# Weights ahead of bias rows in the first head pairs, two modulation chunks moved to the output projection, all copies of values on ScalarE

## The chip, the cores and the metric

One core of one Trainium2 chip runs the kernel. The metric is the device time of one execution in microseconds (us). All times below are in us unless they are marked otherwise. PE is TensorE (matrix products), DVE VectorE, ACT ScalarE, POOL GpSimd and SP SyncE, which here only issues transfers.

## The reference

A decoder trunk of two layers on 256 tokens of width 1024, with fp32 data and fp32 results. Layer 0 mixes tokens with dilated sliding-window attention, layer 1 with chunked gated linear attention; a gated convolutional FFN follows each. Every sub-layer is normalised and modulated by six vectors (shift, scale and gate, twice) that come from the conditioning vector c. The change lies in layer 0's attention:

```python
mod = jax.nn.silu(c) @ w_ada[i] + b_ada[i]
sh1, sc1, g1, sh2, sc2, g2 = [m[:, None, :] for m in jnp.split(mod, 6, axis=-1)]
h = rmsnorm(x, norm_mix[i]) * (1.0 + sc1) + sh1
qkv = (h @ w_in).reshape(B, S, A_GROUPS, 3, A_HEADS, A_HEAD_DIM)
# for each of 3 groups (window, dilation): scores + bias, mask, softmax, times values
wts = jax.nn.softmax(jnp.stack(lses), axis=0)
o = jnp.sum(wts[..., None] * jnp.stack(outs), axis=0)
x = x + g1 * (o.reshape(B, S, A_WIDTH) @ w_out)
```

The 16 heads are taken as 8 head pairs of 2 x 64 columns.

## The kernel before, in words

**Products.** An fp32 product is made of three fp32r products (`mm3`, lines 175 to 177): high part times high part, and the two mixed ones. So each weight tile, a `raw` of up to 128 x 2048 loaded by SyncE (line 159, 1 MB), is split: ScalarE casts the high part (`whi`, line 165), VectorE subtracts it to get the low part (`wlo`, line 169), each in two halves. There are four `raw` buffers and three pairs of split buffers, so a load starts when an older tile's split, or a chunk's dot products, have freed a buffer.

**Modulation chunks.** `next_ada` takes the next of the 40 chunks that are left at this point (`ada_chunk`): a 1 MB load (line 133) into a `raw` buffer, two dot products of 128 x 1024 on VectorE (line 138) and two small activations on ScalarE. The chunks are spread over the kernel: two after the first probabilities, one after each weight tile of queries, and so on.

**Pairs.** Eight tiles of weights hold the queries, keys and values of pair 0 and the queries and keys of pair 1, whose values have two tiles of their own. `evacuate` brings queries (`q`, ScalarE) and keys (`k`, VectorE, group 0 on both) out of PSUM, `by_group` the values `v` in four copies for each half of the tokens: for half 0 all on ScalarE, for half 1 the two big ones (lines 506 and 507) on VectorE. Then for each pair u from 2 on: three tiles of queries and keys (`queries`, PSUM tile `pqk`), two tiles of values (`values`, `pv`), `scores` (`s`), `probabilities` (bias and row maximum on VectorE in line 439, exponentials on ScalarE, normalised `pn` on VectorE), transposes of the four probability tiles (`turn`, `t`, copied to `pt` by ScalarE and VectorE in turn), and `outputs` (`po`, split into `ohi` and `olo`) of the pair before. Bias rows are loaded per pair by eight small transfers (`bias_of`, lines 347 and 348).

**Projection.** `project` multiplies the 8 pairs' outputs by w_out in four tiles (`py`). For the last pair, transposes and outputs stand among the products of the first two tiles (`between`).

**What sets the order.** The code gives each engine's instructions, and a scheduler orders them on each engine by when it expects their inputs; `behind(x)` holds an instruction behind x on its own engine's queue, `tc.issue_after` a transfer behind another. Each engine then runs its queue strictly in that order. SyncE's transfers go round eight semaphores: one that is issued waits for the landing of the one eight places before it. PSUM has eight banks in three tags: "p" two, "s" four, "t" two; `pqk` takes "p", `pv` "p", `s` "s", `t` and `po` "t". For the first two pairs the products take all eight.

Of the kernel before, what the change touches and what calls it, by code (L numbers as in the profile page):

```python
# [57 lines left out]
def trunk(ctx: ExitStack, tc: tile.TileContext, I, out):  # L58
# [337 lines left out]
    with tc.issue_after(last_load[0].ins):  # L396
        nc.sync.dma_start(x_all, I["xT"])
        nc.sync.dma_start(rows_d, rows)
        nc.sync.dma_start(small[:, C_CW:], I["small"][:, C_CW:])
# [59 lines left out]
    def turn(tiles, normed_p, pt):  # L459
        for i in tiles:  # L460
            t = bank("t", "t")
            for j in range(3):
                c = slice(P * j, P * j + P)
                nc.tensor.transpose(t[:, c], normed_p[i][:, c], ident)
            (nc.vector.tensor_copy if i % 2 else nc.scalar.copy)(pt[:, i, :], t[:, 0:KEYS])

# [18 lines left out]

    def evacuate(q, k, g, pq, pk):
# [3 lines left out]
        if g:  # L490
            nc.scalar.mul(q[g], pq, 0.125)
            return nc.vector.tensor_copy(k[g], pk)
# [8 lines left out]
    def by_group(v, pv, n):  # L501


        copy = (nc.scalar.copy, nc.vector.tensor_copy)[n]
# [3 lines left out]
        nc.scalar.copy(v[low, P : 2 * P], pv[top, 2 * P : 3 * P])  # L508
        nc.scalar.copy(v[top, 2 * P : 3 * P], pv[low, P : 2 * P])
# [22 lines left out]
    def queries(u, g, q, k):  # L532
        w = split(I["wqk"][u - 2, g], 2048)
        pqk = bank("pqk", "p")
# [11 lines left out]
    def by_groups(pv):  # L546
        v = [att.tile([P, NG * P], F32, tag=f"v{t}", name="v") for t in range(2)]
        for n in range(2):
            by_group(v[n], pv[n], n)
# [48 lines left out]
    before = probabilities(s, bias)  # L598

    for u in range(2, NPAIR):  # L600
        bias = bias_of(u)
        if u > 2:
            qk = new_qk()
            with behind(last):
                queries(u, 0, *qk)
        middle, end = queries(u, 1, *qk)
        with behind(middle):
            turn((0, 1), *before)
        with behind(end):
            turn((2, 3), *before)  # L610
# [5 lines left out]
        with behind(end):  # L616
# [17 lines left out]
    def project(src, o_of, l, sub, between=None):  # L634
# [32 lines left out]
        for n in range(4):  # L667
# [6 lines left out]
            leave(n, ps)  # L674
        return early
# [491 lines left out]
```

## Time and profile before

| | |
|---|---|
| three runs | 783.54 median, 782.6 to 784.26 |
| profiled execution, its own time | 783.19 |
| its span | 781.4 |
| PE busy | 760.2 (97%) |
| DVE busy | 640.4 (82%) |
| ACT busy | 479.4 (61%) |
| POOL busy | 12.4 (2%) |
| granted TensorE clock, mean of the span | 0.988 |
| bytes moved by DMA, mean rate | 186.30 MB, 238 GB/s |

A row of the timeline gives start, duration, engine, line, operation, the tiles written and read, their shapes and how many instructions it groups; in square brackets stands how long the engine was idle before it, and what ended that. The waits view adds up such idle time by what was waited for: us in total, times, longest. The windows view gives, for a stretch of the span, what each engine was busy, and the granted clock. The chain of waits is the chain of work that ended last, in order of time; SPq is SyncE issuing, DMA a transfer from issue to landing.

### The profile page before, as it was taken

The numbers are of one execution on the slowest core, as the hardware profiler recorded it, in microseconds if no ns is written. First come the engines' busy times: TensorE is split into PE (matmuls) and PEld (weight loads), VectorE is DVE, ScalarE is ACT, GpSimd is POOL, SyncE is SP. The second block draws the span as 40 slices with busy tenths as digits, with TensorE's granted clock in tenths as the row PEclk, the third lists the DMA queues.
The fourth block names the chain that finished last, engine by engine and source line by source line (L and its number), as shares of the span: only waits on it lengthen the run. The fifth ranks groups of instructions, "written<-read, shape, count | busy, mean of one in ns | idle before, by whom it ended". The sixth has DMA issues, their size and how long they took to land.

```text
span 781.4 us, 15909 instructions
## 1 busy us (share of the span) xinstructions
PE 760.2 (97%) x6416; PEld 734.3 (94%) x6416; DVE 640.4 (82%) x1152; ACT 479.4 (61%) x932; POOL 12.4 (2%) x36
## 2 busy tenths in 40 slices
PE   8997989999999999999999999999999999999997
PEld 5996979999999999999999998898999999999996
DVE  6997688788789958999998877797668898899662
ACT  5565455555646657866666656655667866667552
POOL 0000000000000010000000100000010000000000
PEclk9998999999999999999999999999999999999999
DMA  9988685776877746777745993966345665555651
GB/s 348 418 327 311 224 286 167 306 271 242 315 248 277 273 135 244 252 258 244 253 143 196 342 336 135 363 231 230 133 144 183 241 216 174 205 189 210 224 187 55
DMA packets 36200, 186.30 MB, mean 238 GB/s; under 512 B 8412, under 2 KB 10972, under 8 KB 19870
## 3 DMA queue, kind: packets, MB, share of 16 engines
q1 hardware_dynamic: 35744, 184.84, 66.0%
q8 instruction: 50, 0.82, 0.4%
q10 hardware_dynamic: 382, 0.45, 0.2%
q14 instruction: 24, 0.20, 0.1%
HBM read 184.17 MB, written 1.10 MB: 237 GB/s over the span
## 4 chain that ended last, share of the span: by engine, by line
PE 67%; DMA 15%; DVE 13%; ACT 3%; issue 1%; SPq 0%; ACTq 0%; DVEq 0%
PE pab L175 10%; PE pab L176 10%; PE pab L177 10%; DMA raw<-in_wqk 7%; DVE wlo L169 7%; PE pd L175 5%; PE pd L176 5%; PE pd L177 5%; DMA raw<-in_wv 4%; DVE ada_raw L138 3%; PE py L177 2%; PE py L176 2%; PE py L175 2%; ACT whi L165 2%; DMA bias<-rows_d 1%
## 5 line engine op out<-in xcount | busy, mean ns | idle before, releaser
L169 DVE TENSOR_TENSOR wlo<-raw,whi 128x1024 fp32r<-128x1024 f32 (+3 forms) x274 | 291.8, 1098 | 50.5 <-ACT whi L165 49.7
L165 ACT CAST whi<-raw 128x1024 fp32r<-128x1024 f32 (+3 forms) x274 | 245.6, 944 | 116.2 <-PE pab L176 41.3
L177 PE MATMUL pab<-hhi,wlo 128*128 128x256 f32 x672 | 184.9, 276 | 0.0
L176 PE MATMUL pab<-hlo,whi 128*128 128x256 f32 x672 | 184.8, 277 | 0.0
L175 PE MATMUL pab<-hhi,whi 128*128 128x256 f32 x672 | 183.4, 277 | 0.0
L175 PE MATMUL pqk<-hhi,whi 128*128 128x256 f32 x440 | 122.2, 289 | 7.1 <-ACT whi L165 4.2
L177 PEld LDWEIGHTS pab<-hhi,wlo 128*128 128x128 f32 x672 | 126.2, 188 | 0.0
L176 PEld LDWEIGHTS pab<-hlo,whi 128*128 128x128 f32 x672 | 126.0, 188 | 0.2
L175 PEld LDWEIGHTS pab<-hhi,whi 128*128 128x128 f32 x672 | 125.2, 188 | 0.1
L177 PE MATMUL pqk<-hhi,wlo 128*128 128x256 f32 x440 | 122.8, 284 | 1.0 <-DVE wlo L169 1.0
L176 PE MATMUL pqk<-hlo,whi 128*128 128x256 f32 x440 | 122.9, 283 | 0.0
L138 DVE CUSTOM_DVE_ANT_0 ada_raw<-ada_raw,c_bc 128x1024 f32<-128x1024 f32 x96 | 113.6, 1222 | 10.7 <-DMA ada_raw<-in_w_ada 10.7
L176 PE MATMUL pd<-glo,whi 128*128 128x256 f32 x352 | 97.1, 276 | 0.0
L177 PE MATMUL pd<-ghi,wlo 128*128 128x256 f32 x352 | 97.1, 276 | 0.0
L175 PE MATMUL pd<-ghi,whi 128*128 128x256 f32 x352 | 96.8, 276 | 0.0
L175 PEld LDWEIGHTS pqk<-hhi,whi 128*128 128x128 f32 x440 | 83.7, 195 | 8.6 <-ACT whi L165 4.5
L177 PEld LDWEIGHTS pqk<-hhi,wlo 128*128 128x128 f32 x440 | 84.2, 192 | 1.7 <-DVE wlo L169 1.3
L176 PEld LDWEIGHTS pqk<-hlo,whi 128*128 128x128 f32 x440 | 84.4, 192 | 0.1
L176 PEld LDWEIGHTS pd<-glo,whi 128*128 128x128 f32 x352 | 66.1, 188 | 0.0
L177 PEld LDWEIGHTS pd<-ghi,wlo 128*128 128x128 f32 x352 | 66.1, 188 | 0.0
L175 PEld LDWEIGHTS pd<-ghi,whi 128*128 128x128 f32 x352 | 65.9, 188 | 0.0
L728 ACT ACTIVATE r<-pab,small 128x256 f32<-128x256 f32 x86 | 46.7, 558 | 15.5 <-DVE r L731 15.4
(214 smaller groups left out, 1267.3 us busy)
## 6 DMA issues: line engine op xcount, KB each, us to landing
ada_raw<-in_w_ada SPq DMA_DIRECT2D x47, 1024.0 KB, 6.3
raw<-in_w_up SPq DMA_DIRECT2D x42, 1024.0 KB, 4.9
raw<-in_w_down SPq DMA_DIRECT2D x32, 704.0 KB, 5.5
raw<-in_wqk SPq DMA_DIRECT2D x18, 1024.0 KB, 7.8
raw<-in_wv SPq DMA_DIRECT2D x14, 768.0 KB, 4.4
raw<-in_w SPq DMA_DIRECT2D x7, 960.0 KB, 6.4
raw<-in_w_out_a SPq DMA_DIRECT2D x4, 1024.0 KB, 7.3
raw<-in_w_v_b SPq DMA_DIRECT2D x4, 1024.0 KB, 6.1
```

The costliest lines, as they stand in the source:

```text
L138: nc.vector.tensor_tensor_reduce(w, w, c_bc, op0=ALU.mult, op1=ALU.add, scale=1.0, scalar=0.0, accum_out=dot,)
L165: copied[0] = nc.scalar.copy(hi[:, c], raw[:, c])
L169: last_lo[0] = nc.vector.tensor_tensor(lo[:, c], raw[:, c], hi[:, c].bitcast(F32), op=ALU.subtract)
L175: mm(ps, a[0], b[0], start=start, stop=False)
L176: mm(ps, a[0], b[1], start=False, stop=False)
L177: return mm(ps, a[1], b[0], start=False, stop=stop)
L728: nc.scalar.activation(r, u[:, :T], AF.Identity, scale=cw[2], bias=col(C_CB + 44 * l + f))
```

## The change

1. The load of `x` (`x_all` from `xT`, 1 MB) moves from ahead of the first bias rows to behind pair 2's second tile of queries.
2. `by_group` makes all four copies of both halves on ScalarE.
3. After the products of pairs 0 and 1, the values are copied first; then queries and keys are evacuated, pair 0 and pair 1 interleaved.
4. The two chunks after the first probabilities go. Two are added in `project`, one after each of the first two tiles of layer 0's output projection; the 40 chunks keep their sequence, so those in between come two places later.
5. Pair 2's first tile of queries takes a PSUM bank of tag "t", its casts stand behind the last cast of the evacuation on ScalarE, and the bias rows of pairs 1 and 2 are issued behind weight tiles instead of ahead of them. The values of pair 1 are started before the bias rows of pair 0.
6. The transposes of pair 0 are taken in two halves around the scores of pair 1, and the scores of each pair from 2 on stand behind the last transpose.

```diff
-        nc.sync.dma_start(x_all, I["xT"])
...
-    def by_group(v, pv, n):
-        copy = (nc.scalar.copy, nc.vector.tensor_copy)[n]
+    def by_group(v, pv):
+        copy = nc.scalar.copy
...
-    def queries(u, g, q, k):
-        w = split(I["wqk"][u - 2, g], 2048)
-        pqk = bank("pqk", "p")
+    def queries(u, g, q, k, tag="p", after=()):
+        w = split(I["wqk"][u - 2, g], 2048, after=(after, after))
+        pqk = bank("pqk", tag)
...
+    qk0, qk1 = new_qk(), new_qk()
+    v = by_groups(pv)
+    for qk, pqk, g in ((qk0, pqk0, 0), (qk1, pqk1, 0), (qk0, pqk0, 1), (qk0, pqk0, 2), (qk1, pqk1, 1), (qk1, pqk1, 2)):
+        evacuate(*qk, g, pqk[2 * g], pqk[2 * g + 1])
+    pv = [bank("pv", "p") for _ in range(2)]
+    end = values(1, 0, pv)
     bias = bias_of(0)
-    qk0, qk1 = new_qk(), new_qk()
-    for g in range(NG):
-        evacuate(*qk0, g, pqk0[2 * g], pqk0[2 * g + 1])
-    v = by_groups(pv)
-    for g in range(NG):
-        evacuate(*qk1, g, pqk1[2 * g], pqk1[2 * g + 1])
-    pv = [bank("pv", "p") for _ in range(2)]
-    with behind(values(1, 0, pv)):
+    with behind(end):
         s, last = scores(*qk0)
...
-    for n in range(2):
-        next_ada()
-
-    bias = bias_of(1)
+
     qk = new_qk()
     with behind(last):
-        end = queries(2, 0, *qk)
+        end = queries(2, 0, *qk, tag="t", after=last_q)
+    bias = bias_of(1)
     with behind(end[1]):
-        turn(range(4), *before)
+        turn((0, 1), *before)
         s, last = scores(*qk1)
     with behind(last):
+        turn((2, 3), *before)
         outputs(0, v0, before[1])
...
     for u in range(2, NPAIR):
-        bias = bias_of(u)
         if u > 2:
+            bias = bias_of(u)
...
         middle, end = queries(u, 1, *qk)
+        if u == 2:
+            bias = bias_of(u)
+            with tc.issue_after(last_load[0].ins):
+                nc.sync.dma_start(x_all, I["xT"])
...
-            turn((2, 3), *before)
+            turned = turn((2, 3), *before)
...
-        with behind(end):
+        with behind(end, turned):
             s, last = scores(*qk)
...
             leave(n, ps)
+            if n < len(first):
+                next_ada()
```

SyncE's queue in the first pairs, before: the bias rows of pair 0 end, x among them, then two chunks and the first two of eight rows of pair 1, behind which pair 2's first tile of queries (`raw<-in_wqk`) comes.

```order
L348 DMA bias<-rows_d 64x2x64
L397 DMA x_all<-in_xT 128x2048
L347 DMA bias<-rows_d 64x258
L348 DMA bias<-rows_d 64x2x64
L133 DMA ada_raw<-in_w_ada 128x2048 x2
L347 DMA bias<-rows_d 64x258
L348 DMA bias<-rows_d 64x2x64
```

The same place on SyncE, with the change:

```order
L347 DMA bias<-rows_d 64x258
L348 DMA bias<-rows_d 64x2x64
L159 DMA raw<-in_wqk 128x2048
L133 DMA ada_raw<-in_w_ada 128x2048
L347 DMA bias<-rows_d 64x258
L348 DMA bias<-rows_d 64x2x64
```

Pair 2's first tile of queries stands directly behind pair 0's bias rows, with one chunk behind it (the chunk that belongs to that tile); before, eight bias rows of pair 1, two chunks and x stood ahead of it. x now stands behind the second tile.

VectorE while pairs 0 and 1 are evacuated, before: keys, two copies of values among them, then a chunk's dot products and the first probabilities.

```order
L492 COPY k<-pqk 128x256
L506 COPY v<-pqk 64x256
L507 COPY v<-pqk 64x2x128
L492 COPY k<-pqk 128x256
L495 SCALAR_TENSOR_TENSOR q<-pqk,q 128x256
L492 COPY k<-pqk 128x256
L499 TENSOR_TENSOR k<-pqk,k 128x256
L492 COPY k<-pqk 128x256
L499 TENSOR_TENSOR k<-pqk,k 128x256
L138 ISA ada_raw,dot<-ada_raw,c_bc 128x1024
```

The same place on VectorE, with the change:

```order
L497 SCALAR_TENSOR_TENSOR q<-pqk,q 128x256
L494 COPY k<-pqk 128x256
L501 TENSOR_TENSOR k<-pqk,k 128x256
L494 COPY k<-pqk 128x256
L169 TENSOR_TENSOR wlo<-raw,whi 128x1024 x2
L501 TENSOR_TENSOR k<-pqk,k 128x256
L438 ISA prob,m<-s,bias 128x384
```

The copies of values and the dot products are gone from here, and the split of pair 2's first tile (`wlo`, 128x1024) stands ahead of the last key (pair 1, group 0) and of the probabilities. The dot products now follow the third tile's split, some 20 rows later.

TensorE in the output projection, at the outputs of the last pair (`po`); `py` 3452 and 3461 are the first two tiles of the projection, 3623 is the third, `ohi` 3569 and `olo` 3570 are the last pair's outputs. Before:

```order
L475 MATMUL po_3556<-pt_3443,v_3405 64x64 x4
L177 MATMUL py_3461<-ohi_2996,wlo_3465 128x256
L175 MATMUL py_3461<-ohi_3368,whi_3464 128x256
L176 MATMUL py_3461<-olo_3369,whi_3464 128x256
L177 MATMUL py_3461<-ohi_3368,wlo_3465 128x256
L175 MATMUL py_3461<-ohi_3368,whi_3464 128x256
```

With the change (the numbers are others; `ohi` 3549 and `olo` 3550 are the last pair's outputs here):

```order
L475 MATMUL po_3536<-pt_3423,v_3385 64x64 x4
L175 MATMUL py_3432<-ohi_3549,whi_3435 128x256
L175 MATMUL py_3441<-ohi_3549,whi_3444 128x256
L176 MATMUL py_3432<-olo_3550,whi_3435 128x256
L177 MATMUL py_3432<-ohi_3549,wlo_3436 128x256
L175 MATMUL py_3432<-ohi_3549,whi_3435 128x256
```

Before, 19 products of other pairs follow the outputs, ahead of the first that reads `ohi` of the last pair; with the change that one follows at once, and the 19 stand ahead of the outputs. The transposes of the last pair stand after 62 products instead of 24, and the four dot products of the two chunks stand on VectorE among the last pair's probabilities. After the first two tiles of the projection all engines run the same sequence as before.

More of the change, by code (lines that the diff above doesn't have):

```diff
@@ L463, in turn @@
                 c = slice(P * j, P * j + P)
-                nc.tensor.transpose(t[:, c], normed_p[i][:, c], ident)
+                last = nc.tensor.transpose(t[:, c], normed_p[i][:, c], ident)
             (nc.vector.tensor_copy if i % 2 else nc.scalar.copy)(pt[:, i, :], t[:, 0:KEYS])
+        return last
     def outputs(u, v, pt):
@@ L507, in by_group @@
         copy(v[low, :].rearrange("p (g x) -> p g x", g=3)[:, ::2, :], pv[low, 0 : 3 * P].rearrange("p (g x) -> p g x", g=3)[:, ::2, :])
-        nc.scalar.copy(v[low, P : 2 * P], pv[top, 2 * P : 3 * P])
-        nc.scalar.copy(v[top, 2 * P : 3 * P], pv[low, P : 2 * P])
+        copy(v[low, P : 2 * P], pv[top, 2 * P : 3 * P])
+        copy(v[top, 2 * P : 3 * P], pv[low, P : 2 * P])
     def new_qk():
```

5 lines of the change are left out of this document (3 added, 2 removed).

## The prediction

> **What bounds the kernel now.** I read the windows view first: who is busy from pair 3 on (120 to 260 us), around it, and in the output projection (260 to 300).
>
> ```profile
> 110.00:120.00 10.00, 7.27 (x82) 6.09 (x81) 7.39 (x18) 5.09 (x8) 0.20 (x2) 0.67 0.72 267
> 120.00:260.00 140.00, 138.61 (x1254) 134.34 (x1253) 118.64 (x236) 80.33 (x179) 0.59 (x6) 1.00 0.73 264
> 260.00:300.00 40.00, 40.00 (x365) 37.86 (x364) 29.57 (x62) 24.43 (x55) 2.38 (x2) 1.00 0.53 189
> ```
>
> The columns after the window's length are PE, PEld, DVE, ACT and POOL, then the granted clock. TensorE bounds both long windows: 1.39 us idle in 140, none in 40. In the ten microseconds before, it is idle for 2.73 and its clock is 0.67. So time can only come from stalls ahead of 120 us. The waits view names them:
>
> ```profile
> PE pqk L175 <- ACT whi L165: 4.2, 1, 4.2
> PE po L471 <- ACT v L509: 2.7, 1, 2.7
> PE pqk L177 <- DVE wlo L169: 1.0, 1, 1.0
> ```
>
> The first and third are one stall, A; the second is stall B. TensorE's timeline around A, the 48 pqk matmuls of pair 2's first weights:
>
> ```profile
> 69.34 0.34 PE L177 MATMUL pv<-whi,hlo 128*128 128x384 f32 x1
> 73.88 0.58 PE L175 MATMUL pqk<-hhi,whi 128*128 128x256 f32 x1 [4.20 <-ACT whi L165]
> 79.01 0.41 PE L177 MATMUL pqk<-hhi,wlo 128*128 128x256 f32 x1
> 79.50 0.28 PE L177 MATMUL pqk<-hhi,wlo 128*128 128x256 f32 x1
> 82.67 0.28 PE L177 MATMUL pqk<-hhi,wlo 128*128 128x256 f32 x1
> ```
>
> The 27 steps from 79.50 to 82.67 take 0.117 each, so 48 take 5.6; from the last pv's end (about 69.5) to that of the last pqk (82.67 + 0.12 = 82.8) are 13.3. A costs 7.7: 4.2 + 1.0 of waiting and 2.5 of half clock (a matmul lasts 0.41 before 79.2, 0.28 after). Its cause stands in SyncE's timeline and the chain of waits:
>
> ```profile
> 52.16 0.33 SPq L397 DMA_DIRECT2D x_all<-in_xT  x1
> 53.74 1.07 SPq L133 DMA_DIRECT2D ada_raw<-in_w_ada  x2
> 65.86 0.60 SPq L348 DMA_DIRECT2D bias<-rows_d  x1
> 66.56 0.54 SPq L159 DMA_DIRECT2D raw<-in_wqk  x1
> ...
> 55.34 10.96 DMA bias<-rows_d
> 67.67 9.02 DMA raw<-in_wqk
> 77.84 2.29 DVE wlo L169 x2
> 80.12 5.57 DMA raw<-in_wqk
> 103.87 6.79 DMA raw<-in_wqk
> ```
>
> Pair 2's first weights are issued only at 66.56, because SyncE stands at a bias row until 65.86, behind three 1 MB loads (x, two chunks).
>
> Stall B, VectorE and then TensorE, with an undisturbed output group at 93.58 for comparison:
>
> ```profile
> 111.81 1.23 DVE L169 TENSOR_TENSOR wlo<-raw,whi 128x1024 fp32r<-128x1024 f32 x1 [2.65 <-ACT whi L165]
> 112.96 0.41 DVE L506 COPY v<-pv 64x256 f32<-64x256 f32 x1
> 113.38 0.43 DVE L507 COPY v<-pv 64x256 f32<-64x256 f32 x1
> 113.84 0.56 DVE L465 COPY pt<-t 128x384 f32<-128x384 f32 x1
> ...
> 114.54 1.97 PE L471 MATMUL po<-pt,v 128*64 128x256 f32 x8 [2.73 <-ACT v L509]
> 117.30 0.58 PE L175 MATMUL pqk<-hhi,whi 128*128 128x256 f32 x1
> 120.24 0.29 PE L176 MATMUL pqk<-hlo,whi 128*128 128x256 f32 x1
> ...
> 93.58 1.08 PE L471 MATMUL po<-pt,v 128*64 128x256 f32 x8
> 95.06 0.38 PE L177 MATMUL pqk<-hhi,wlo 128*128 128x256 f32 x1
> ```
>
> The view blames ScalarE's v, but what outputs read is pt, and its last piece is VectorE's copy at 113.84, queued behind a split (wlo) whose load landed at 110.66 (103.87 + 6.79) and two copies of values. B costs 2.73, plus 1.28 for the outputs (2.76 against 1.48), plus 1.3 for 13 pqk (2.94 against 0.22 + 12 x 0.117): 5.3.
>
> The trace thus halves the clock after 2.73 us of idling. The Trainium skill, "TensorE: Matmul & The Clock Gate", section "What's actually happening", wants an idle window of about 3.4 us for that. By it B would be worth 2.73 alone and the forecast 2.6 us later; the rows at 114.54 and 117.30 disagree, so I use 5.3.
>
> **The change part by part.** *Loads.* x and one bias set leave the way: the first weights follow the eighth bias row (about 53.25; the rows at 52.16 and 53.74 stand there now) and land, at the 5.57 of the load at 80.12, at 58.8. The chunks' four products (1.2 each) leave VectorE's queue ahead of the probabilities. The second weights wait for a bias row behind the chunk (an estimate of 62.8: the 53.74 at which a chunk is issued now, plus the 9.02 that the load at 67.67 takes in traffic) and land near 68.4, 5.57 later. So the split is ready before the last pv ends and A's 7.7 go. What is late next is a new wait:
>
> ```profile
> 60.92 0.37 ACT L498 CAST k<-pqk 128x256 fp32r<-128x256 f32 x1
> 72.80 1.99 ACT L165 CAST whi<-raw 128x1024 fp32r<-128x1024 f32 x2
> 63.71 0.98 PE L419 MATMUL s<-k,q 64*128 64x256 f32 x12
> ```
>
> *New wait at the first scores (price 1.0).* The fourth score tile takes the PSUM bank of qk1's group 0, which is free after VectorE's last k. That now stands behind the split of pair 2's weights. ScalarE ends its evacuations at 61.3 now (60.92 + 0.37); the two big copies that come over add an estimated 0.72 (they take 0.84 on VectorE), and the k cast, now behind the split, takes 0.37 off: 61.65. Casts end at 63.65 (1.99); the two splits (2.29) run from the first half's cast, to 65.0; k takes 0.42, as the like-sized subtraction olo does (280.61, below): 65.4. TensorE gets there at 64.4 (63.71 plus three tiles of four of the 0.98). Bounds: 0 if the two halves overlap better, and 1:1 above when the load lands after 61.65.
>
> *Stall B.* The copies of values leave VectorE (0.41 + 0.43), and the feeding moves up. Pair 3's second weights, issued at 103.87 now, would go out at 90.6 if they kept the 13.3 by which the first weights move (66.56 to 53.25), and at 97.1 if they moved with TensorE alone (by A less the new wait, 6.7). I take 93.9: half of the issues on the way wait for splits, which move up with the loads, and half for products and probabilities, which follow TensorE. At 6.79 they land at 100.7; cast, split and pt copy (1.05, half of the 2.29, and 0.56) end at 103.5. TensorE reaches the outputs at 70.5 (69.5 + 1.0) + 5.6 + 29.0 (from 82.8 to 111.81, where its wait begins now) = 105.1. So there is no wait, with a margin of 1.6, and the gain is 5.3; at the late bound the pt copy comes 1.6 after TensorE.
>
> *Edits with one answer.* The bank of its own for pair 2's first queries keeps them from waiting for the copies of values; the transposes in two halves and the scores behind the last of them only reorder TensorE's work. One of these transposes needs a pt copy that stands on ScalarE behind the cast of the third weights: 0 to 0.5 if that load is late, taken as 0.
>
> *ScalarE's copies.* About 0.72 us per pair go to an engine that is busy 80.33 of 140, 0.84 leave one busy 118.64 of 140. Taken as nothing: TensorE hides both. Without the cover, 0.72 a pair, 4.3 in six.
>
> *Chunks in the projection.* Two chunks (2 MB, four products) come among the last pair's probabilities and shift the transposes from after 24 py to after 62.
>
> ```profile
> L138 DVE CUSTOM_DVE_ANT_0 ada_raw<-ada_raw,c_bc x96: 1206/1222/1237, 8.8 to 746.8; 128x1024 f32<-128x1024 f32 x96
> ...
> DMA to landing us min/median/max: 4.7/6.6/11.4
> ...
> 279.52 0.63 PE L475 MATMUL po<-pt,v 128*64 128x64 f32 x16
> 280.61 0.42 DVE L481 TENSOR_TENSOR olo<-po,ohi 128x256 fp32r<-128x256 f32 x1 [4.31 <-ACT ohi L480]
> ```
>
> 4 x 1.22 = 4.9 on VectorE, hidden by the later transposes (38 py x 0.117 = 4.4) and VectorE's 4.31 of idling; uncovered, they cost 4.9. But outputs now stand directly ahead of the py that read them (19 others were between): TensorE must wait for olo, which ends at 281.03, 0.9 after the outputs end (280.1); two py (0.23) fit in. Price 0.7, between 0 and 0.9.
>
> **Sum.** Against the profiled execution's 783.19 (span 781.4 and 1.8 around it; the median of three runs is 0.35 higher): -7.7 + 1.0 - 5.3 + 0.7 = -11.3, less 0.3 for the idle time that the smaller lead (below) may add: -11.0, so 772.2, and 772.5 as a median. Its own range is 769 (without the new waits, 1.7, the 0.3 and the 1.39 of idle time) to 774 (the late transpose and half of the smaller lead).
>
> **The rivals.** *Late first weights.* The load shares the queues with bias rows and a chunk; if it takes the 10.96 of the bias rows it lands at 64.2, the new wait grows by 2.55 and the clock halves (2.5 as in A): 777.5. Against: x no longer runs beside it. Chance 0.11.
>
> *Feeding binds.* The chain of waits from 117 to 259 runs over loads and splits, hardly TensorE:
>
> ```profile
> 128.57 4.43 DMA raw<-in_wv
> 250.72 4.30 DMA raw<-in_wv
> ...
> 207.66 0.39 PE L175 MATMUL pqk<-hhi,whi 128*128 128x256 f32 x1
> 237.33 0.39 PE L175 MATMUL pqk<-hhi,whi 128*128 128x256 f32 x1
> ```
>
> Its period is 30.54 ((250.72 - 128.57) / 4), TensorE's 29.67 (237.33 - 207.66). The loads come 10.0 earlier, TensorE 12.0 (7.7 - 1.0 + 5.3), so the lead shrinks by 2.0, and TensorE waits that much more (0.3 of it is in the forecast) if the 0.84 taken from VectorE doesn't shorten the loop: 774.2. Chance 0.13.
>
> *B stays: the change doesn't do what it says.* The margin at pair 2's outputs is 1.6; with the late bound and the 9.02 of the load at 67.67, pt is 1.6 + 2.2 = 3.8 late, the clock halves as it does now, and all of B is back: 777.8. Against: the feeding has a head start of 13.3. Chance 0.09.
>
> *Slower: ScalarE blocks itself.* The copies of both halves now stand behind the cast of the next pair's first weights, in order. Where that load lands late, pt, v and the banks of values wait too; each time costs one B, 5.3. It decides from three pairs (15.9, over the gain of 11.0: 788.4); in five it gives 799.0. Against: half of the copies stand there already and TensorE idled 1.39 in those pairs. Chance 0.05.
>
> All three of the middle cases at once (5.05 + 1.7 + 5.3 on 772.5) give 784.6, no change that can be told: 0.02.
>
> **The numbers.** Forecast 0.60; faster 0.93, same 0.02, slower 0.05, where 0.2%, 1.6 us, is about what a measurement of this kernel can tell from no change. The range, 769 to 778, holds the forecast and the three middle rivals, and leaves out 0.07 and its edges.
>
> **What would show it.** Right: TensorE has no wait of 4.2 at 69.5 and pqk starts there at full clock; a wait of about 1 on VectorE's k near 64.4; outputs near 105 without a wait, 110 to 120 at clock 1.00; 0.7 after the last pair's outputs. Wrong: the first wqk landing after 62, waits on whi or wlo in pairs 3 to 7, a clock below 1.00 there, or py waiting for pn or wlo.

## The result, and the profile after

The change makes the kernel faster by some 7 us: 776.31 is the median of six runs (774.47 to 777.02) against 783.19 of six runs of the kernel before (782.59 to 787.83). The ratio is 0.990, with a 95% interval from 0.9874 to 0.9925. A second measurement, among the experiments, gave 774.91 and 0.9912 (0.9896 to 0.9928). The forecast was 772.5; the gain has the predicted sign, its largest part has the predicted cause, and it is about two thirds of the predicted size. The profiled execution took 777.02, the slowest of its six, with a span of 775.1. One execution of one kernel below was disturbed (1409.07, at a granted clock of 0.828) and is left out of its median.

The waits view of the kernel after, TensorE alone:

```profile
PE t L463 <- ACT pt L464: 4.3, 4, 2.6
...
PE po L471 <- DVE pt L464: 0.9, 1, 0.9
PE pv L175 <- DVE k L494: 0.8, 1, 0.8
PE s L418 <- DVE k L501: 0.8, 1, 0.8
PE py L175 <- ACT ohi L480: 0.5, 1, 0.5
```

The waits of 4.2 and 1.0 of stall A have no successor here, and the 2.7 at the outputs has become 0.9. There are two predicted small waits (`s` 0.8, `py` 0.5), and one that was taken as nothing: 2.6 for a copy by ScalarE of a transposed tile. I call it stall C. The windows view of the kernel after (columns as in the prediction):

```profile
72.00:83.00 11.00, 8.80 (x105) 8.23 (x103) 5.93 (x14) 7.77 (x21) 0.20 (x2) 1.00 0.76 245
83.00:87.00 4.00, 3.55 (x18) 3.56 (x19) 4.00 (x12) 0.77 (x3) 0.00 (x0) 0.57 0.85 356
...
110.00:120.00 10.00, 10.00 (x101) 9.86 (x98) 9.19 (x27) 5.54 (x13) 0.00 (x0) 1.00 0.60 211
120.00:252.00 132.00, 129.52 (x1181) 125.17 (x1181) 109.30 (x213) 79.45 (x178) 0.60 (x6) 1.00 0.75 271
```

From 110 to 120 TensorE is full at clock 1.00, where it had 7.27 of 10 at 0.67. Between 30 and 300 us the clock is down at one place only, 83 to 87 (0.57), behind C. In the pairs, 120 to 252, it idles 2.48 of 132, where it idled 1.39 of 140. TensorE's timeline of the kernel after at the places of the sum:

```profile
64.13 0.97 PE L418 MATMUL s<-k,q 64*128 64x256 f32 x9
65.86 0.59 PE L418 MATMUL s<-k,q 64*128 64x258 f32 x3 [0.76 <-DVE k L501]
71.29 0.28 PE L175 MATMUL pqk<-hhi,whi 128*128 128x256 f32 x1
83.45 0.90 PE L463 MATMUL t<-ident,pn 128*128 128x128 f32 x3 [2.65 <-ACT pt L464]
109.27 1.08 PE L471 MATMUL po<-pt,v 128*64 128x256 f32 x8 [0.86 <-DVE pt L464]
110.75 0.39 PE L175 MATMUL pqk<-hhi,whi 128*128 128x256 f32 x1
260.76 0.28 PE L175 MATMUL py<-ohi,whi 128*128 128x256 f32 x1
275.44 0.50 PE L175 MATMUL py<-ohi,whi 128*128 128x256 f32 x2 [0.48 <-ACT ohi L480]
287.08 0.59 PE L302 MATMUL early<-early_x,raw 128*128 128x257 f32 x2
```

The same two marks at the end of the attention, in the kernel before (first product of the projection, first of the FFN):

```profile
268.23 0.28 PE L175 MATMUL py<-ohi,whi 128*128 128x256 f32 x1
...
293.24 1.03 PE L302 MATMUL early<-early_x,raw 128*128 128x257 f32 x4
```

From these marks and those of the prediction, the two profiled executions differ by stages as follows.

| stage (ends at) | before | after | difference | forecast |
|---|---|---|---|---|
| start to first scores | 63.71 | 64.13 | +0.4 | 0 |
| first scores to pqk of pair 2 | 5.8 | 7.16 | +1.35 | +1.0 |
| the 48 pqk, waits in them | 13.3 | 5.65 | -7.6 | -7.7 |
| to ready for pair 2's outputs | 29.0 | 31.5 | +2.5 | 0 |
| outputs with wait, and slow pqk behind them | 5.5 + 1.3 | 2.3 | -4.5 | -5.3 |
| pairs 3 to 7 (to the first py) | 149.6 | 150.0 | +0.4 | +0.3 |
| projection (to the FFN) | 25.0 | 26.3 | +1.3 | +0.7 |
| rest | 488.2 | 488.0 | -0.1 | 0 |
| sum, against the spans' 781.4 and 775.1 | | | -6.3 | -11.0 |

As in the prediction, pair 2's outputs are the ones taken in pair 2's round; they belong to pair 1. "Ready" is where the wait at the outputs begins: 111.81 before, 109.27 - 0.86 = 108.41 after; the 1.3 are the slow pqk of stall B. Half of the missing 4.7 is the row with C. C itself cost more than this row shows: 2.65 of waiting and about 1.5 for the half clock behind it (83.45 to 86.67 took 3.2 instead of 1.7). Where the stage won some 1.6 of that back is open. C's chain, as the chain of waits of the kernel after shows it, and then ScalarE's timeline there:

```profile
66.86 13.68 DMA raw<-in_wqk
```

```profile
80.62 1.99 ACT L165 CAST whi<-raw 128x1024 fp32r<-128x1024 f32 x2 [3.11 <-DMA raw<-in_wqk]
...
82.92 0.47 ACT L464 COPY pt<-t 128x384 f32<-128x384 f32 x1
```

The third weights of pair 2 land 13.68 after their issue. ScalarE stands at their cast for 3.11, and the copy that frees the bank of transposes is queued behind it (82.92). One of the two banks of that tag is held by pair 2's first queries (edit 5), so TensorE can't take the other transpose until 83.45. SyncE's timeline of the kernel after says why the weights come late, and why pair 3's do too:

```profile
54.54 0.54 SPq L159 DMA_DIRECT2D raw<-in_wqk  x1
...
61.18 0.45 SPq L347 DMA_DIRECT2D bias<-rows_d  x1
64.59 0.60 SPq L348 DMA_DIRECT2D bias<-rows_d  x1
65.28 0.54 SPq L159 DMA_DIRECT2D raw<-in_wqk  x1
65.92 0.38 SPq L133 DMA_DIRECT2D ada_raw<-in_w_ada  x1
66.35 0.42 SPq L610 DMA_DIRECT2D x_all<-in_xT  x1
66.86 0.63 SPq L159 DMA_DIRECT2D raw<-in_wqk  x1
...
99.33 0.33 SPq L159 DMA_DIRECT2D raw<-in_wqk  x1
```

The first weights go out at 54.54 instead of 66.56. But the bias rows that used to stand ahead of them now stand between them and the second weights: the last two of these rows start at 61.18 and 64.59, after gaps of 1.9 and 3.0 in which SyncE waits for the landing of the transfer eight places before (the first weights and a chunk), and the second weights follow at 65.28, with a chunk, x and the third weights, 3 MB more, issued within 1.6 us of them.

### The profile page after: what moved, and what is told of

It is laid out like the page before. It is cut to its first block, busy times and chain, and to the rows that moved or that the text cites. A ratio compares the mean times of both kernels' runs of the same rounds, so it can differ in the third digit from the quotient of the medians.

```text
span 775.1 us, 15908 instructions
## 1 busy us (share of the span) xinstructions
PE 755.9 (98%) x6416; PEld 731.5 (94%) x6416; DVE 633.7 (82%) x1136; ACT 484.7 (63%) x948; POOL 12.4 (2%) x36
## 4 chain that ended last, share of the span: by engine, by line
PE 71%; DMA 12%; DVE 11%; ACT 3%; issue 1%; SPq 0%; DVEq 0%; ACTq 0%
PE pab L176 10%; PE pab L175 10%; PE pab L177 10%; DMA raw<-in_wqk 8%; DVE wlo L169 5%; PE pd L175 5%; PE pd L177 5%; PE pd L176 5%; DMA raw<-in_wv 3%; PE pqk L175 3%; PE pqk L176 2%; DVE ada_raw L138 2%; PE pqk L177 2%; PE py L175 2%; PE py L176 2%; PE py L177 2%
## 5 line engine op out<-in xcount | busy, mean ns | idle before, releaser
L169 DVE TENSOR_TENSOR wlo<-raw,whi 128x1024 fp32r<-128x1024 f32 (+3 forms) x274 | 291.8, 1098 | 62.8 <-ACT whi L165 62.1
L177 PE MATMUL pd<-ghi,wlo 128*128 128x256 f32 x352 | 97.1, 276 | 0.0
L176 PE MATMUL pd<-glo,whi 128*128 128x256 f32 x352 | 97.1, 276 | 0.0
```

Source lines behind the costliest of these rows:

```text
L169: last_lo[0] = nc.vector.tensor_tensor(lo[:, c], raw[:, c], hi[:, c].bitcast(F32), op=ALU.subtract)
L176: mm(ps, a[0], b[1], start=False, stop=False)
L177: return mm(ps, a[1], b[0], start=False, stop=stop)
```

## The experiments

Theory: the missing gain is what the new waits show, at `s`, at C, at pair 2's outputs and in the projection; take one away, and its time comes back. Rival: the feeding (loads, casts, splits) sets when pairs 3 to 7 can end, so that a wait taken away comes back as another. The table gives medians; the ratio is to the kernel before, measured with the kernels of the same group; po, py and FFN are the marks of pair 2's outputs, the first py and the first product of the FFN, in one profiled execution each. Medians of different groups are compared by their ratios.

| kernel | median (lowest to highest) | ratio, 95% | po | py | FFN |
|---|---|---|---|---|---|
| change, first time | 776.31 (774.47 to 777.02) | 0.9900, 0.9874 to 0.9925 | 109.27 | 260.76 | 287.08 |
| change, again | 774.91 (774.11 to 776.96) | 0.9912, 0.9896 to 0.9928 | 108.61 | 259.50 | 285.42 |
| x behind the third weights | 777.50 (775.14 to 778.16) | 0.9927, 0.9908 to 0.9947 | 107.71 | 260.28 | 286.19 |
| first pt on VectorE | 775.12 (773.25 to 779.44) | 0.9910, 0.9885 to 0.9934 | 107.30 | 258.89 | 284.81 |
| chunks in the FFN | 774.14 (772.39 to 776.03) | 0.9891, 0.9871 to 0.9912 | 109.88 | 258.81 | 283.96 |
| split behind the last key | 777.03 (775.12 to 778.20) | 0.9926, 0.9905 to 0.9947 | 108.62 | 260.89 | 286.81 |
| x behind pair 5's weights | 776.64 (775.05 to 779.75) | 0.9939, 0.9918 to 0.9959 | 107.96 | 261.15 | 287.07 |
| all four | 777.20 (776.11 to 781.48) | 0.9946, 0.9925 to 0.9967 | 108.18 | 261.15 | 286.30 |
| copies on VectorE | 779.90 (775.40 to 781.49) | 0.9964, 0.9947 to 0.9981 | 106.59 | 259.86 | 286.60 |
| all four, products left out | 778.45 (777.31 to 780.06) | 0.9951, 0.9933 to 0.9969 | 108.01 | 262.75 | 287.90 |
| all four, loads left out | 816.73 (815.32 to 817.95) | 1.0446, 1.0414 to 1.0479 | | | |
| pt on VectorE, chunks in the FFN | 773.90 (771.90 to 774.62) | 0.9888, 0.9863 to 0.9913 | | | |
| before, with two moves only | 773.93 (771.89 to 775.13) | 0.9894, 0.9871 to 0.9917 | 103.59 | 256.26 | 283.00 |

**Stall C: x behind the third weights.**

```diff
         if u == 2:
             bias = bias_of(u)
-            with tc.issue_after(last_load[0].ins):
-                nc.sync.dma_start(x_all, I["xT"])
...
         queries(u, 2, *qk)
+        if u == 2:
+            with tc.issue_after(last_load[0].ins):
+                nc.sync.dma_start(x_all, I["xT"])
```

> One transfer moved: the 1 MB load of x is issued behind pair 2's third weights instead of ahead of them. Theory (the transposes' wait of 2.65 at 83.45 comes from the third weights landing at 80.55, 13.68 after their issue, with a chunk and x ahead of them, 3.3 per MB from 70.52, and from the pt copy that stands behind their cast on ScalarE): they land near 77.2, cast until 79.2, pt by 80.1, TensorE gets there at 80.6: no wait, no half clock, about 4.0 faster than the changed kernel's 776.3, so 772.3. Rival one (the landing is set by buffers or the semaphore of an older transfer, not by x): landing and time as in the changed kernel. Rival two (what is behind the weights now, the bias rows of pair 2 and x, becomes late): the wait at 83.45 goes and one of like size appears at probabilities or outputs by 110, 775 or more.

Measured: 777.50, no gain on the change (0.9927 against 0.9900 and 0.9912, intervals that overlap). C is gone; TensorE's timeline of this kernel shows what stands in its place:

```profile
81.65 0.55 PE L463 MATMUL t<-ident,pn 128*128 128x128 f32 x3 [1.06 <-DVE k L501]
91.47 0.52 PE L463 MATMUL t<-ident,pn 128*128 128x128 f32 x3 [1.09 <-DVE pn L453]
155.85 0.87 PE L463 MATMUL t<-ident,pn 128*128 128x128 f32 x6 [1.74 <-DVE pt L464]
```

Two waits of about 1 us in pair 2, and one of 1.74 in pair 4. The outputs of pair 2 begin 1.56 earlier than in the change (107.71 against 109.27), the first py 0.48 earlier than in the first profile of the change, and 0.78 later than in the second. What C gave back is lost again: for the rival.

**Stall C: the first pt copy on VectorE,** which is idle there.

```diff
-            (nc.vector.tensor_copy if i % 2 else nc.scalar.copy)(pt[:, i, :], t[:, 0:KEYS])
+            (nc.vector.tensor_copy if i % 2 == odd else nc.scalar.copy)(pt[:, i, :], t[:, 0:KEYS])
...
-        turn((0, 1), *before)
+        turn((0, 1), *before, 0)
```

> One copy changes its engine: of pair 0's first two transposed tiles, VectorE copies the first and ScalarE the second (the other way round in the changed kernel). The loads stay as they are. Theory (the wait is for the pt copy behind a cast in ScalarE's queue, VectorE stands idle from 76.7 to 81.7): third weights still land at 80.5, the first pt copy is made near 77.6, the second transpose runs without a wait over 0.5 and at full clock, about 4.0 faster than 776.3: 772.3. Rival (the third weights themselves are needed by then, so the wait only moves to pqk): a wait of 2 or more at the third pqk tile or at the next transpose, 775 to 776.

Measured: 775.12, as the change by its intervals. TensorE's timeline of this kernel at C, and at the outputs of the first pair:

```profile
82.82 0.55 PE L463 MATMUL t<-ident,pn 128*128 128x128 f32 x3 [0.67 <-ACT pt L464]
...
92.64 0.65 PE L471 MATMUL po<-pt,v 128*64 128x256 f32 x4 [1.59 <-DVE pt L464]
```

C shrinks from 2.65 to 0.67 and the clock stays full; a wait of 1.59 comes at the next outputs. The py mark is 1.87 earlier than in the first profile of the change, 0.61 than in the second. The third weights are as late as before (their cast starts at 79.98), so the chain of C is shown to be the one told above. By these marks its worth is below 2, not 4.

**The new wait at the first scores: the low half of the split behind the last key.**

```diff
-        end = queries(2, 0, *qk, tag="t", after=last_q)
+        end = queries(2, 0, *qk, tag="t", after=(last_q[0], last_k[2]), low=(last_k[3],))
```

> Only the order on two engines: the cast of pair 2's first weights on ScalarE and their split on VectorE are held behind the last key of the evacuation (pair 1, group 0). Theory (the first scores wait 0.76 for that key behind the split, 1.35 with the restart): the wait at 65.86 goes, splits end 0.5 later, well before 71.3: about 1.3 faster, 775.0. Rival (the delay of the split is passed on to the second weights' cast and the probabilities, and so to pqk at 71.3 or the transposes): less than 0.5 gained, 776 or above.

Measured: 777.03. The wait at `s` is gone and pqk begins at 70.00 instead of 71.29, so this wait cost 1.3, as the row of the table above says. But at pair 2's outputs TensorE of this kernel waits longer:

```profile
108.62 2.45 PE L471 MATMUL po<-pt,v 128*64 128x256 f32 x7 [2.64 <-DVE pt L464]
```

2.64 instead of 0.86, with half the clock behind it (0.50 from 108 to 114 in the windows view); py comes at 260.89, 0.13 later than with the change. For the rival again.

**The projection: the two chunks in the FFN instead.**

```diff
             leave(n, ps)
-            if n < len(first):
-                next_ada()
...
-                if l == 0 and i % 5 == 4 and i < 20:
+                if l == 0 and (i % 5 == 4 and i < 20 or i in (7, 12)):
```

> The two chunks leave the output projection for the FFN of layer 0 (one each at its 8th and 13th tile), so their sequence stays and each still comes in time. Theory (the chunks cost the projection 1.3: later transposes, outputs directly ahead of the products that read them): the stretch from the first py to the first early matmul is back from 26.3 to 25.0, about 1.3 faster than 776.3: 775.0. Rival (the FFN has no room: each chunk is 1 MB and 2.4 of VectorE): the projection gets faster by 1.3 and the FFN slower by as much, 776.3 or above.

Measured: 774.14. The projection takes 25.15 (258.81 to 283.96) instead of 26.32, so the chunks cost 1.2 there, and nothing where they are now (behind the FFN mark 488.1, before the change 488.2). That one is for the theory: behind the last pair nothing takes the time back. Up to the loads of the projection this kernel runs the same instructions in the same order on every engine as the change, yet it needs 148.9 from pair 2's outputs to py, the change 151.5. So part of what the change's first profile shows in pairs 3 to 7 belongs to that execution.

**The change again,** with no edit.

> The changed kernel, unedited, a second time beside the next three. Theory (the feeding of pairs 3 to 7 nearly ties with TensorE, so that small shifts decide whether transposes wait there): its times spread over 2 or more as they did (774.5 to 777.0), and the profile shows the first pairs as before (waits of about 0.8 at 66, 2.6 at 83.4, about 1 at the outputs near 109), while the waits in pairs 4 to 7 may be 0 or up to 2.5 together. Rival (those waits belong to the kernel and not to the execution): the waits of 0.66, 0.56, 0.45 and 0.81 stand at the same places again.

Measured: 774.91; its profiled execution, 776.96, is again the slowest of its six. In it the same stretch takes 150.9; TensorE's waits of 0.66 and 0.56 at 155 and 187 are not there, and the one at pair 2's outputs is 1.92 instead of 0.86. So executions of one program differ by 1 to 2 us in which of the near-tied waits appear, and a single profile of this kernel can't price one below that. Nor does stall B come out as small: here 1.92 of waiting, 1.05 more for the outputs (108.61 to 111.14, against 1.48) and 0.5 more for the first pqk make 3.5, against 5.3 before the change.

**x behind pair 5's third weights,** so that no extra MB stands among the loads of pairs 2 and 3.

```diff
         queries(u, 2, *qk)
+        if u == 5:
+            with tc.issue_after(last_load[0].ins):
+                nc.sync.dma_start(x_all, I["xT"])
```

> One transfer moved far: x is loaded behind pair 5's third weights, so that nothing of it lies between 66 and 85. Theory (x delays the third weights by 3.3 and with them values' weights and pair 3's weights, the feeding that decides outputs near 109; moving it behind only these weights gave the delay to the next loads): third weights land near 77.2, pair 3's second weights are issued near 96.5 instead of 99.3, no wait of 2.65 at 83.4, none at the outputs, TensorE reaches pair 3 about 4 to 5 earlier: 771.5 to 772.5. Rival (the feeding is limited by splits and products on VectorE and ScalarE, not by bytes): pair 3's second weights are issued at 98 or later and the time stays at 775 or above. Pair 5 gets 1 MB more; its transposes may wait up to 1.

Measured: 776.64, py at 261.15. The waits are others (1.43 and 1.06 near 80, 1.83 at 156), and TensorE's waits between 60 and 262 add up to 6.3, where the two profiles of the change have 6.8 and 5.9. One MB less in the way isn't what the feeding lacks.

**All four edits together:** x behind pair 5's weights, the pt copy on VectorE, the split behind the key, the chunks in the FFN.

> All edits that the parts spoke for together: x behind pair 5's third weights, the first pt copy of pair 0 on VectorE, the first split behind the last key, the two chunks in the FFN instead of the projection. Theory: first scores' wait gone (1.3), transposes' wait gone (about 4), projection 1.2 shorter, outputs near 104 to 105 without a wait: 6 below the changed kernel's 776.3, 769 to 771. Rival (what TensorE gains ahead of pair 3 is taken back by the feeding): pairs 3 to 7 lose 2 to 4 in waits of the transposes for pt, and the time is 773 to 775, no better than with the chunks alone moved.

Measured: 777.20, slower than the chunks alone (ratios 0.9946 and 0.9891, intervals that don't meet). The profiled execution, 776.11, is the fastest of its six, so it need not hold all that slows the others. VectorE's timeline of this kernel, and TensorE's behind it:

```profile
78.36 2.36 DVE L169 TENSOR_TENSOR wlo<-raw,whi 128x1024 fp32r<-128x1024 f32 x2 [2.54 <-ACT whi L165]
80.64 0.55 DVE L464 COPY pt<-t 128x384 f32<-128x384 f32 x1
```

```profile
81.24 0.86 PE L463 MATMUL t<-ident,pn 128*128 128x128 f32 x3 [4.49 <-DVE pt L464]
```

Here the pt copy, moved to VectorE, stands behind a split that waits for the third weights' cast: the blocking copy has only changed its engine, and TensorE waits 4.49.

**The same, with twelve dot products of pairs 3 and 4 left out** (the loads stay; these modulation values are not computed).

```diff
-            nc.vector.tensor_tensor_reduce(
-                w, w, c_bc, op0=ALU.mult, op1=ALU.add, scale=1.0, scalar=0.0, accum_out=dot,
-            )
+            if left_out:
+                nc.vector.tensor_copy(dot, w[:, 0:1])
+            else:
+                nc.vector.tensor_tensor_reduce(...)
```

> As the run before, but the loads of the six chunks stay and their twelve products on VectorE are left out (12 x 1.22, 14.6 in two pairs; the result is not the reference's). Theory of bytes: the wait near 156 stays at 1 or more and the projection starts within 0.7 of 261.15. Rival (VectorE's products, which stand in its queue ahead of splits and of the pt copies, limit the feeding): the wait is gone and the projection starts at 258.5 or less. If both this run and the one before do that, the feeding is a loop in which either relief is enough.

Measured: 778.45, no faster than with them (777.20; ratios 0.9951 and 0.9946), with some 14 us of VectorE's work gone (12 x 1.22). So VectorE's dot products in those two pairs are not what binds.

**The same, with the loads of six chunks left out** (their products stay, on other data).

```diff
-        for i in range(dmas):
+        for i in range(0 if left_out else dmas):
```

> All edits of the last kernel together, and the loads of the six modulation chunks of pairs 3 and 4 are left out (their products run on other data, so that VectorE's and ScalarE's work and the buffers stay; the result is not the reference's). Theory (the feeding that takes the first pairs' gain back at pair 4 is limited by the bytes of a pair, 4.5 MB of weights and 3 MB of chunks, and the waits for their landing): the transposes' wait of 1.8 near 156 is gone, the six outputs of pairs 3 to 7 stand 29.3 apart, and the projection starts 2.5 or more earlier than the 261.15 of the last kernel, at 258.5 or less: 773 to 774. Rival (the products on VectorE limit it): wait and projection stay within 0.7 of the last kernel's.

Measured: 816.73, slower by 4.5%. The windows view of this kernel:

```profile
110.00:125.00 15.00, 9.07 (x58) 8.58 (x58) 8.35 (x19) 4.65 (x11) 0.00 (x0) 0.77 0.14 48
125.00:150.00 25.00, 17.36 (x98) 15.65 (x97) 13.10 (x19) 10.11 (x18) 0.00 (x0) 0.76 0.37 108
```

The DMA engines are nearly idle (0.14 and 0.37) while TensorE waits, by the waits view 15.0 us at `pqk` for the cast of weights that come late. The edit changed when the weights' loads are issued, so it says nothing on whether their bytes bind. It does show what weights that come late cost: some 40 us (816.73 against 777.20).

**The two big copies of the second half back on VectorE.**

```diff
-        copy = nc.scalar.copy
+        copy = (nc.scalar.copy, nc.vector.tensor_copy)[n]
```

> One part of the change undone: the two big copies of the second half's values go back to VectorE; order of evacuation, loads and chunks stay as in the changed kernel. Theory (stall B went because pair 3's weights come about 4.5 earlier, not because the copies left VectorE): the outputs near 109 wait 0.8 longer than the changed kernel's 0.9, about 1.7, at full clock; the first scores' wait shrinks by up to 0.7, since ScalarE reaches the casts earlier; in all within 1 of 776.3. Rival (the copies on VectorE were the cause of B): a wait of 2.7 or more at the outputs with the clock at half, 780 or more.

Measured: 779.90 in twelve runs, 5.0 above the change measured beside it, and the intervals of the ratios don't touch. So with the change's other edits, ScalarE's copies are worth about 5. Where they are won I can't show: the profiled execution of this kernel took 776.57, the second fastest of its twelve, and has no wait at pair 2's outputs (106.59), where the prediction had put them.

**The first pt copy on VectorE and the chunks in the FFN.**

> Two edits of the changed kernel together: VectorE makes the first pt copy of pair 0, and the two chunks are in the FFN instead of the projection; x stays behind the second tile. Theory (each of the two showed its gain alone, 2.3 at the end of the projection for the first and 3.1 for the second, of which 1.2 belong to the projection and the rest differs between executions): the projection ends 2 to 4 earlier than the changed kernel's 287.1 and 285.4, the time is 773 to 774.5, the best of all. Rival (the feeding takes the first edit's gain back): as with the chunks alone moved, 774.1, or worse.

Measured: 773.90 in five runs, as with the chunks alone (774.14). No trace of it is read here.

**The kernel before, with two moves only:** x behind pair 2's second tile, the first two chunks in the projection. Bias rows stay ahead of the weights, evacuation, copies, bank and transposes as before.

```diff
     with tc.issue_after(last_load[0].ins):
-        nc.sync.dma_start(x_all, I["xT"])
...
-    for n in range(2):
-        next_ada()
...
         middle, end = queries(u, 1, *qk)
+        if u == 2:
+            with tc.issue_after(last_load[0].ins):
+                nc.sync.dma_start(x_all, I["xT"])
...
             leave(n, ps)
+            if n < len(first):
+                next_ada()
```

> One part of the change alone, on the kernel before: x is loaded behind pair 2's second tile of queries and the two chunks after the first probabilities go to the projection. The bias rows of pair 1 stay ahead of the weights, the evacuation, the copies on VectorE, the PSUM bank and the transposes are as before. Theory (stall A is the wait of SyncE for three 1 MB landings): the first weights are issued near 59 and land by 65, A falls from 7.7 to 1 or less, and the time is 774.5 to 777.5, as with the whole change. Rival (without the order of evacuation and the copies on ScalarE the first casts, or the outputs near 107, are late): a wait of 2.7 or more remains at one of the two places with a halved clock, 779 to 782.

Measured: 773.93, ratio 0.9894 (0.9871 to 0.9917): these two moves alone bring the whole gain of the change, within the intervals. SyncE's timeline of this kernel:

```profile
58.92 0.54 SPq L159 DMA_DIRECT2D raw<-in_wqk  x1
...
60.02 0.38 SPq L159 DMA_DIRECT2D raw<-in_wqk  x1
```

The first weights go out 4.4 later than with the change (58.92 against 54.54), the second 5.3 earlier (60.02 against 65.28), since no bias row stands between them. TensorE, and then VectorE at pair 2's outputs:

```profile
70.13 0.39 PE L175 MATMUL pqk<-hhi,whi 128*128 128x256 f32 x1 [1.40 <-ACT v L508]
...
103.59 1.08 PE L470 MATMUL po<-pt,v 128*64 128x256 f32 x8
...
256.26 0.28 PE L175 MATMUL py<-ohi,whi 128*128 128x256 f32 x1
```

```profile
97.17 0.54 DVE L464 COPY pt<-t 128x384 f32<-128x384 f32 x1
97.64 2.34 DVE L169 TENSOR_TENSOR wlo<-raw,whi 128x1024 fp32r<-128x1024 f32 x2
102.17 0.42 DVE L505 COPY v<-pv 64x256 f32<-64x256 f32 x1 [2.19 <-PE pv L177]
...
104.80 2.36 DVE L169 TENSOR_TENSOR wlo<-raw,whi 128x1024 fp32r<-128x1024 f32 x2 [1.77 <-ACT whi L165]
```

A is gone but for 1.40 of waiting for a bank, which the change's own bank avoids. At the outputs there is no wait, although the copies of values (the first at 102.17) are still on VectorE, and although pair 3's second weights are split only from 104.80, after the outputs have begun. By these rows the reason is the place of the last pt copy: at 97.17 it stands ahead of pair 3's first split (97.64), where the kernel before and the change have it behind the first half of the second split. VectorE's timeline of the change:

```profile
107.52 1.23 DVE L169 TENSOR_TENSOR wlo<-raw,whi 128x1024 fp32r<-128x1024 f32 x1 [2.52 <-ACT whi L165]
108.66 0.55 DVE L464 COPY pt<-t 128x384 f32<-128x384 f32 x1
```

So stall B is a matter of what pt is queued behind. The moves led the scheduler to take the last transposes earlier, and no copy had to leave VectorE for that. The other traces agree but for one. In the four kernels where the last pt copy stands ahead of pair 3's second split (x behind the third weights, first pt on VectorE, x behind pair 5's weights, all four) TensorE doesn't wait at these outputs; where it stands behind the split's first half (both profiles of the change, chunks in the FFN, split behind the key) it waits 0.86 to 2.64. The exception is the kernel with the copies on VectorE: pt stands behind that half there too, but the split starts at 104.50 instead of 107.52, and there is no wait. Yet the four kernels that are rid of the wait reach py at 258.89 to 261.15, no earlier than the others (258.81 to 260.89). So the place of pt cures stall B, but it isn't shown to be what brings the two moves to py at 256.26.

From its outputs to py this kernel then takes 152.7, 3.7 more than the kernel with the chunks in the FFN: of a lead of 6.3 at pair 2's outputs (103.59 against 109.88), 2.55 are left at py. That is again the pattern of the rival.

What the feeding waits for is not settled, and that it is the feeding that takes the time back is argued from this pattern, not shown by a run that makes it faster. VectorE's dot products in pairs 3 and 4 are excluded, one MB less among the first loads doesn't help, and the run without the loads is no test. Two combinations were not tried: the two moves with the chunks in the FFN, and the first pt copy on VectorE on top of them.

## Why the prediction was right, and where it was not

*Direction and stall A: right.* The first weights are issued at 54.54 (forecast 53.25) and are there before they are needed, pqk starts at 71.29 without a wait and at full clock, and the 48 matmuls take 5.65. Forecast -7.7, measured -7.6. The kernel with two moves shows that removing x and the chunks is enough for all of it but 1.40; putting the weights ahead of the bias rows wasn't needed.

*New wait at the first scores: right in place and cause, 1.35 instead of 1.0.* TensorE waits 0.76 and comes to pqk 1.35 later than before. Taking the wait away moved pqk by 1.3.

*"One of these transposes needs a pt copy that stands on ScalarE behind the cast of the third weights: 0 to 0.5 if that load is late, taken as 0": this step failed.* It measured 2.65 of waiting and about 1.5 for the half clock behind it, 2.5 net in the table. The prediction gives no sum for its 0 to 0.5, which fits a load of the usual length (5.57); the third weights took 13.68, more than twice that, because SyncE issued them behind the second weights, a chunk and x within 1.6 us, the second weights at 65.28 instead of the estimated 62.8. The condition was named, the load's place in the queue was not looked at.

*Stall B: reduced, by 4.5 in the first profile and by 1.8 in the second (3.5 left of 5.3) instead of by all of 5.3, and by another way than argued.* I had the split and pt end at 103.5, ahead of TensorE at 105.1, because pair 3's second weights would be issued at 93.9, at the latest at 97.1. They went out at 99.33, and pt ends at 109.21, 0.8 after TensorE is ready at 108.41. So the lead that I counted on did not come: the bias rows moved from ahead of the first weights to ahead of the second, and passed the delay on (61.18 to 65.28). That the wait is 0.86 and not longer I put down to two things. C had made TensorE late as well; the second profile bears this out, where C doesn't halve the clock, TensorE is ready at 106.69, 1.7 earlier, and waits 1.92. And the two copies of values (0.41 and 0.43 before) no longer stand between the split and pt; that is by the rows alone, for with the copies back on VectorE they stand behind pt (at 107.24). In the kernel whose split follows the key, TensorE comes earlier, waits 2.64, and loses the clock: with 2.2 more for the outputs and 1.1 more for the pqk behind them, all of B is back there (5.9 against 5.3). So the small wait of the first profile was in part luck. The two moves show a full cure of the wait: pt ahead of that split.

*The projection: right mechanism, 1.3 instead of 0.7.* There is the wait of 0.48 for the last outputs (by the row for their high part, `ohi`); the kernel with the chunks in the FFN gives 1.2 of the 1.3 back. That wait is gone there too, so what the order costs and what the chunks' products cost, which I had taken as hidden, is not told apart.

*ScalarE's copies: no cost, as forecast;* with the change's other edits they are worth 5.0, though in the two moves' kernel nothing is lost without them.

*The rivals.* "Feeding binds", at 774.2, is the nearest to the medians (776.31 and 774.91), and the experiments bear its pattern out: four edits that took one wait away, alone or together, each brought another, and py stayed between 258.8 and 261.2 in all kernels with the change that compute everything. My forecast added up stalls as if each saved its length. That the loads and splits are what takes the time back, as the rival says, stays argued. "Late first weights" fell: their cast starts at 61.92 in ScalarE's timeline, directly behind the evacuation, forecast 61.65. A relative of "ScalarE blocks itself" appeared once, as C: a copy behind the cast of a late load, but a pt copy and not one of values, and it didn't repeat from pair to pair. The total miss is 4.7 in the profiled execution and 3.8 in the first median (2.4 in the second).

## What to carry to other kernels

When a move lets one load go earlier, read the queue that is left behind it: transfers moved out of its way stand in the way of the next one, and a small copy behind that next load's cast can hold TensorE. Where a wait stands behind a late load, ask first which instruction the reader truly needs and what it is queued behind; moving that one ahead of the split took this wait away. Then look whether the end comes earlier too: here it mostly didn't. Where loads, splits and TensorE run nearly tied, the saved stalls are an upper bound for the gain, and the smallest part of a large change should be run alone before the rest is added.

## What the runs showed of the hardware

The clock doesn't go by the length of the gap alone. TensorE's timeline of the second run of the change:

```profile
83.02 0.55 PE L463 MATMUL t<-ident,pn 128*128 128x128 f32 x3 [2.53 <-ACT pt L464]
...
83.53 0.28 PE L175 MATMUL pqk<-hhi,whi 128*128 128x256 f32 x1
...
108.61 1.74 PE L471 MATMUL po<-pt,v 128*64 128x256 f32 x8 [1.92 <-DVE pt L464]
...
111.73 0.41 PE L177 MATMUL pqk<-hhi,wlo 128*128 128x256 f32 x1
```

After 2.53 of idling the matmuls last 0.28, the full clock; after 1.92 they last 0.41 until 112.2, the half clock. In the first run 2.65 at the same place as the 2.53 did halve it. The Trainium skill, "TensorE: Matmul & The Clock Gate", section "What's actually happening", tells of a free-running window of about 3.4 us after which an idle array is throttled. That nearly the same gap halves the clock in one execution and not in the next agrees with a window that runs free; that 1.92 was enough doesn't agree with one that must be idle from end to end.

The traces' record of the granted clock shows such a grid. Within one execution, the stretches at half clock begin whole multiples of 3.413 us apart: at 21.26, 72.46 and 113.42 before the change (15 and 12 multiples), at 21.76 and 83.20 after it (18). They last 3.41 (after C) or 6.83 (after A and after B). On this grid the 2.65 of the first run has 2.39 within one step, and the clock is halved at its end. The 2.53 of the second run is cut into 1.09 and 1.43, and the 2.84 at the same place in the kernel with the copies on VectorE into 1.00 and 1.84 (its own half clock begins at 21.95); neither halves it. The 1.92 lies in one step. But the idle time in a step doesn't decide alone either: ahead of stall B's half clock a step had 1.61. Half a clock for 3.41 cost about 1.5 after C.

A load's time depends on what was issued just ahead of it: 13.68 for a 1 MB load behind three others, where the prediction's undisturbed row has 5.57.
